# Delta rule: q and k of two head pairs projected channel-major together, their values token-major in 512 columns and convolved over tokens by shifted copies

## The chip, the cores and the metric

The kernel runs on one core of one Trainium2 chip. The time is the device time of one execution in microseconds (us), as the median of three runs. The engines are TensorE (PE in the profile, with PEld for its weight loads), VectorE (DVE), ScalarE (ACT), GpSimd (POOL) and SyncE (SP), which issues nearly all DMAs.

## The reference

One decoder layer on 256 tokens and 2048 channels, in float32. Two branches, a gated delta rule (GDN) and an mLSTM, are projected from the same `h`, gated, merged and projected out. What the change touches is the first part of the GDN branch:

```python
h = rms_norm(x, norm_pre_w) * (1 + scale) + shift
proj = h @ w_in                                   # (256, 2048) @ (2048, ...)
def causal_conv_silu(x, w):                       # 4 taps over tokens, per channel
    xp = jnp.pad(x, ((0, 0), (3, 0), (0, 0)))
    return silu(sum(xp[:, j:j + s] * w[j] for j in range(4)))
qkv = causal_conv_silu(gdn_qkv, gdn_conv_w)       # 8192 channels: q 16x128, k 16x128, v 32x128
q_a = l2_normalize(q) * 128 ** -0.5 ; k_a = l2_normalize(k)   # each shared by two value heads
g_log = -exp(A_log) * softplus(a + dt_bias) ; beta = sigmoid(b)
o_a = gated_delta_rule(q_a, k_a, v_a, g_log, beta)
o_a = rms_norm(o_a, gdn_norm_w) * silu(gdn_z)
```

## The kernel before

**Projections.** Every product in float32 is made of three float32r products: both operands are split into a high and a low part (`whi`, `wlo` of the weights, `h_hi`, `h_lo` of the tokens), and `mm3` issues high*high, high*low and low*high (L231). ACT casts the high part (L169), DVE subtracts for the low part (L170; in the start GpSimd does some). The weights stream through `Stream`: units of 1 MB (`raw`, 3 buffers, loaded by SP at L164), each split in two pieces of 1024 columns (`whi`, `wlo`, 4 buffers each). A piece is split up to four pieces ahead of its use on PE.

There are two forms. `add_proj_t` (PSUM tiles `pt`) gives channels on partitions: the weights are the stationary operand and the 256 tokens move, so a group of 512 columns of `w_in` takes 16 chunks x 4 x 3 = 192 matmuls of 128x256. `add_proj_n` (tiles `pn`) gives tokens on partitions: the tokens are stationary and 512 weight columns move, 16 x 2 x 3 = 96 matmuls of 128x512 for a group of the same size. Either group has four units, so eight pieces.

**The GDN stage** has 8 periods (`gdn_period`), each of two head pairs. A pair is one key head and two value heads, and its 512 columns (q, k, v, v) are one group of `w_in`. A period projects pair 0 with `add_proj_t`, the gates z of four heads with `add_proj_n`, and pair 1 with `add_proj_t`.

**Side work.** Everything else is written as Python generators in `side`; after each piece on PE `side.step()` lets every generator issue its next portion, so a `yield` is one piece. A budget (`side.debt`, `side.room`) spreads DVE work. Each engine works its own instructions in the order in which they were issued. The generators of a period:

- `gdn_stage1` per pair: `conv_silu` convolves the four channel blocks in place in `qs` (ACT scales the last tap at L650, DVE adds three shifted taps each at L656, ACT Silu at L659); q and k are split (`qh`, `ql`); the decay rows are loaded (`gb`, L674) and masked on GpSimd (`dd`, L681); PE makes the scores `psa` and `psb`, transposes q into `psb` (L715) and the two value heads into `psv` (L720) so that tokens come on partitions; DVE scales the scores into `au` (L748); ACT scales the values out of `psv` into `rr` (L761).
- `base_inverse` per period: the unit lower triangles are inverted in 32x32 blocks, by a chain of small DVE instructions (`tmp`, `xx`, L799 to L805) between DMA round trips through DRAM (`ud`, `ug`, `xd`, `xcmp`).
- `gdn_stage2` per period, about a period later: products with the inverse, the output, its norm and gate, the transposes back, and the store to `o_dr`.

Of the kernel before, what the change touches and what calls it, by code (L numbers as in the profile page):

```python
# [117 lines left out]
def hybrid_layer_kernel(  # L118
# [402 lines left out]
    def gates(ps):  # L521
# [53 lines left out]
        yield from wait(3)  # L575
# [34 lines left out]

    def add_proj_t(g, after, extra=None):

        st_ = {}
        for t in range(4):
# [9 lines left out]
            stream.add(w_in[g][:, t * 2048:(t + 1) * 2048], prep_w, use, after=  # L624
# [4 lines left out]
    def add_proj_n(g, after, extra=None):  # L629

        st_ = {}
        for t in range(4):
            def use(h, hi, lo, t=t):
                if t == 0 and h == 0:
                    st_["ps"] = [jtile(f"pn{i}") for i in range(2)]
                for kc in range(2):
                    k = t * 4 + h * 2 + kc
                    o = kc * 512
                    for b in range(2):
                        mm3(st_["ps"][b], h_hi[:, k, b * P:(b + 1) * P], h_lo[:, k, b * P:(b + 1) * P],  # L640
                            hi[:, o:o + 512], lo[:, o:o + 512], k == 0, k == KC - 1)
            stream.add(w_in[g][:, t * 2048:(t + 1) * 2048], prep_w, use, after=
                       (lambda: after(st_["ps"])) if t == 3 else None)
            if extra:
                extra()

    def conv_silu(ps, taps, dst, hi=None, late=0):
# [3 lines left out]
        yield from wait(1 + late)  # L651
# [8 lines left out]
        if hi is not None:  # L660
            A.copy(hi, dst[:, 0:2])
# [31 lines left out]
    def gdn_stage1(p, ps, res):  # L693

        z = p % 2
        qs = bp.tile([P, 4, S], F32, name="qs", tag="qs")
        qh = bp.tile([P, 2, S], F32R, name="qh", tag="qh", bufs=1)
        yield from conv_silu(ps, lambda n, j: late_c["gcv"][:, (p * 4 + n) * 4 + j:(p * 4 + n) * 4 + j + 1], qs, qh,
                             0 if z else 3)
        gb = decay_rows(2 * p)  # L700
        dd = decay_mask(gb)
        b12 = bp.tile([P, 2], F32, name="b12", tag="b12")
        G.tensor_tensor(b12, gb[:, :, P - 1], ngt[:, 0, 2 * p:2 * p + 2], op=ALU.add)
        side.debt += 0.7
        ql = bp.tile([P, 2, S], F32R, name="ql", tag="ql", bufs=1)
        V.tensor_tensor(ql, qs[:, 0:2], qh.bitcast(F32), op=ALU.subtract)
        yield from wait(2)
        yield from banks(3)
        res["t"] = side.t
        psa = gtile("psa", True)  # L710
        mm3(psa, qh[:, 1, 0:P], ql[:, 1, 0:P], qh, ql, True, True)
        psb = gtile("psb", True)
        mm3(psb[:, 0:256], qh[:, 1, P:S], ql[:, 1, P:S], qh[:, :, P:S], ql[:, :, P:S], True, True)
        for m in range(2):
            T.transpose(psb[:, 256 + m * P:256 + (m + 1) * P], qs[:, 0, m * P:(m + 1) * P], ident)  # L715
        psv = gtile("psv", True)
        side.debt -= 1.6
        for blk in range(2):
            for h in range(2):
                T.transpose(psv[:, (blk * 2 + h) * P:(blk * 2 + h + 1) * P],  # L720
                            qs[:, 2 + h, blk * P:(blk + 1) * P], ident)
# [6 lines left out]
        if z == 0:
            res["eq"] = bp.tile([P, 2, 2], F32, name="eq", tag="eq", bufs=3)
            res["rr"] = bp.tile([P, 2, 2, S], F32, name="rr", tag="rr")  # L730
        rk = bp.tile([P, 2], F32, name="rk", tag="rk")
        cj = bp.tile([P, 2, 2], F32, name="cj", tag="cj")
        res["au", z] = au = bp.tile([P, 2, 768], F32, name="au", tag="au", bufs=5)

        side.debt += 1.3
        for blk, ps_, n, c0 in ((0, psa, 256, 0), (1, psb, 128, 512)):
            V.scalar_tensor_tensor(au[:, 0, c0:c0 + P], ps_[:, n:n + P], 1.0, ident, op0=ALU.mult, op1=ALU.mult,
                                   accum_out=sse[:, 2 + blk:3 + blk])
        V.tensor_scalar(sse[:, 2:4], sse[:, 2:4], EPS, None, op0=ALU.add)
        V.reciprocal(rk, sse[:, 2:4])  # L740
        V.tensor_tensor(cj, tt[:, :, 32 + 2 * p:34 + 2 * p], rk.unsqueeze(2).broadcast_to([P, 2, 2]), op=ALU.mult)
        V.tensor_scalar(res["eq"][:, z], sse[:, 0:2], EPS, 128.0 * EPS, op0=ALU.add, op1=ALU.mult)

        for blk, ps_, n, c0 in ((0, psa, 256, 0), (1, psb, 128, 512)):
            yield
            side.debt += 1.45 if blk == 0 else 1.0
            for h in range(2):
                V.scalar_tensor_tensor(au[:, h, c0:c0 + 2 * n].rearrange("p (a b) -> p a b", a=2),  # L748
                                       ps_[:, 0:2 * n].rearrange("p (a b) -> p a b", a=2), cj[:, blk, h:h + 1],
                                       dd[:, h, c0 // 2:c0 // 2 + n].unsqueeze(1).broadcast_to([P, 2, n]),  # L750
                                       op0=ALU.mult, op1=ALU.mult)
            gfree(ps_)
            if blk == 0:
                sk = bp.tile([P, 2], F32, name="sk", tag="sk")
                pow_(sk, sse[:, 2:4], phalf[:, 0:2])
            else:
                scored[0] = p
        block_rows(res, z)
# [16 lines left out]
    def base_inverse(zg, res, zr):  # L775
# [48 lines left out]
        while zg < 7 and side.t < res["t"] + STAGE2_STEPS - 1:  # L824
# [142 lines left out]
    def period_tail(zg, ps, res, zr):  # L967
        yield from gdn_stage1(2 * zg + 1, ps, res)
        yield
        side.add(base_inverse(zg, res, zr), 2)  # L970

# [502 lines left out]
```

## Time and profile before

| what | value |
|---|---|
| median of three runs | 1596.39 us (1596.14 to 1596.67) |
| span of the profiled execution, first to last instruction | 1595.6 us |
| the profiled execution's own time beside its span | not given apart; the median lies 0.8 us above the span |
| PE / PEld / DVE / ACT / POOL busy | 99 / 87 / 72 / 59 / 15% |
| GDN stage | from 336.9 to 991.5 us, in steady state 81.62 us a period |
| memory traffic | 372.37 MB, mean 233 GB/s |

The durations of matmuls in the profile overlap, since matmuls are pipelined: a sum of them is more than the time that they take, and the distance from start to start tells their pace. A queue's letter q after an engine's name (SPq) marks DMAs issued by it.

### The profile page before, as it was taken

The numbers are of one execution on the slowest core, as the hardware profiler recorded it, in microseconds if no ns is written. First come the engines' busy times: TensorE is split into PE (matmuls) and PEld (weight loads), VectorE is DVE, ScalarE is ACT, GpSimd is POOL, SyncE is SP. The second block draws the span as 40 slices with busy tenths as digits, with TensorE's granted clock in tenths as the row PEclk, the third lists the DMA queues.
The fourth block names the chain that finished last, engine by engine and source line by source line (L and its number), as shares of the span: only waits on it lengthen the run. The fifth ranks groups of instructions, "written<-read, shape, count | busy, mean of one in ns | idle before, by whom it ended". The sixth has DMA issues, their size and how long they took to land.

```text
span 1595.6 us, 25488 instructions
## 1 busy us (share of the span) xinstructions
PE 1581.1 (99%) x9854; PEld 1388.9 (87%) x9854; DVE 1145.7 (72%) x1804; ACT 937.7 (59%) x1496; POOL 244.8 (15%) x204
## 2 busy tenths in 40 slices
PE   8999999999999999999999999999999999999998
PEld 5888888899999999999999999889988888888886
DVE  6786556765689788888878888775768766756654
ACT  7754446765666575757576766665566554444443
POOL 4787761000000010000000000000000000100100
PEclk9999999999999999999999999999999999999999
DMA  9998775965555546555646455546778878776573
GB/s 379 390 385 324 267 296 179 298 233 182 187 192 186 190 151 202 172 184 172 195 157 206 155 193 177 187 165 228 280 271 306 321 277 294 282 249 236 207 270 111
DMA packets 96067, 372.37 MB, mean 233 GB/s; under 512 B 26021, under 2 KB 45877, under 8 KB 58185
## 3 DMA queue, kind: packets, MB, share of 16 engines
q1 hardware_dynamic: 95848, 370.65, 65.7%
q8 instruction: 77, 1.26, 0.3%
q14 instruction: 44, 0.36, 0.1%
q0 software_dynamic: 96, 0.09, 0.0%
q10 hardware_dynamic: 2, 0.01, 0.0%
HBM read 354.40 MB, written 16.31 MB: 232 GB/s over the span
## 4 chain that ended last, share of the span: by engine, by line
PE 82%; issue 13%; ACT 1%; DMA 1%; POOL 1%; DVE 1%; SPq 0%; DVEq 0%; POOLq 0%; ACTq 0%
PE pn L231 37%; PE pt L231 28%; PE py L231 8%; POOL mg L1264 1%; PE psa L231 1%; PE mq L871 1%; PE mz L880 1%; ACT whi L169 0%; DVE wlo L170 0%; DMA gb<-rows 0%; PE csil L301 0%; PE po L921 0%; PE po L920 0%; PE pa L892 0%; PE pc L910 0%
## 5 line engine op out<-in xcount | busy, mean ns | idle before, releaser
L170 DVE TENSOR_TENSOR wlo<-raw,whi 128x1024 fp32r<-128x1024 f32 x453 | 555.9, 1235 | 266.5 <-ACT whi L169 265.2
L169 ACT CAST whi<-raw 128x1024 fp32r<-128x1024 f32 x516 | 532.2, 1046 | 308.5 <-PE pn L231 156.3
L231 PE MATMUL pt<-h_hi,whi 128*128 128x256 f32 x1280 | 367.8, 287 | 0.0
L231 PE MATMUL pt<-h_hi,wlo 128*128 128x256 f32 x1280 | 362.1, 283 | 0.0
L231 PE MATMUL pt<-h_lo,whi 128*128 128x256 f32 x1280 | 362.0, 283 | 0.0
L231 PE MATMUL pn<-whi,h_hi 128*128 128x512 f32 x896 | 353.0, 394 | 0.9 <-ACT part L474 0.6
L231 PE MATMUL pn<-wlo,h_hi 128*128 128x512 f32 x896 | 349.2, 390 | 0.9 <-POOL wlo L170 0.9
L231 PE MATMUL pn<-whi,h_lo 128*128 128x512 f32 x896 | 349.1, 390 | 0.0
L231 PEld LDWEIGHTS pt<-h_hi,whi 128*128 128x128 f32 x1280 | 245.3, 192 | 1.4
L231 PEld LDWEIGHTS pt<-h_lo,whi 128*128 128x128 f32 x1280 | 245.4, 192 | 0.3
L231 PEld LDWEIGHTS pt<-h_hi,wlo 128*128 128x128 f32 x1280 | 245.2, 192 | 0.0
L231 PEld LDWEIGHTS pn<-whi,h_hi 128*128 128x128 f32 x896 | 168.3, 188 | 36.4 <-ACT part L474 1.5
L231 PEld LDWEIGHTS pn<-wlo,h_hi 128*128 128x128 f32 x896 | 168.3, 188 | 35.8 <-POOL wlo L170 1.7
L231 PEld LDWEIGHTS pn<-whi,h_lo 128*128 128x128 f32 x896 | 168.2, 188 | 35.3 <-DVE h_lo L170 0.2
L170 POOL TENSOR_TENSOR wlo<-raw,whi 128x1024 fp32r<-128x1024 f32 (+1 forms) x63 | 145.7, 2319 | 50.5 <-ACT whi L169 50.4
L231 PE MATMUL py<-whi,yhi 128*128 128x512 f32 x384 | 150.6, 392 | 0.0
L231 PE MATMUL py<-whi,ylo 128*128 128x512 f32 x384 | 149.6, 390 | 0.0
L231 PE MATMUL py<-wlo,yhi 128*128 128x512 f32 x384 | 149.4, 389 | 0.0
L472 DVE TENSOR_TENSOR part<-pn,part 128x512 f32<-128x512 f32 x112 | 73.7, 685 | 45.5 <-PE pn L231 45.4
L169 ACT CAST yhi<-ya 128x512 fp32r<-128x512 f32 x48 | 29.9, 622 | 127.1 <-PE py L231 110.5
L656 DVE SCALAR_TENSOR_TENSOR qs<-pt,gcv,qs 128x255 f32<-128x255 f32 (+2 forms) x192 | 92.0, 479 | 4.6
L170 DVE TENSOR_TENSOR ylo<-ya,yhi 128x512 fp32r<-128x512 f32 x48 | 33.2, 691 | 74.2 <-ACT yhi L169 74.2
(267 smaller groups left out, 1807.0 us busy)
## 6 DMA issues: line engine op xcount, KB each, us to landing
raw<-in_dram SPq DMA_DIRECT2D x259, 1024.0 KB
ar<-in_dram SPq DMA_DIRECT2D x31, 1024.0 KB
raw<-in_dram SPq DMA_DIRECT2D x16, 512.0 KB
ya<-o_dr SPq DMA_DIRECT2D x32, 256.0 KB
gate_dr<-part SPq DMA_DIRECT2D x11, 512.0 KB
gb<-rows SPq DMA_DIRECT2D x20, 256.0 KB
raw<-in_dram SPq DMA_DIRECT2D x6, 768.0 KB
ug<-ud SPq DMA_DIRECT2D x32, 128.0 KB
```

What stands on the lines that cost most here:

```text
L169: A.copy(hi, src)
L170: (eng or V).tensor_tensor(lo, src, hi.bitcast(F32), op=ALU.subtract)
L231: T.matmul(ps, l, r, start=start and i == 0, stop=stop and i == 2, skip_group_check=True)
L472: V.tensor_tensor(part[g][:, b], ps[b], part[g][:, b], op=ALU.add)
L656: V.scalar_tensor_tensor(dst[:, n, sh:], src[:, 0:S - sh], taps(n, 3 - sh), dst[:, n, sh:], op0=ALU.mult, op1=ALU.add)
L871: T.matmul(psp[64:128, m * 64:(m + 1) * 64], um(m)[0:64, 64:128], y0[:, m], start=True, stop=True)
L880: T.matmul(psz[0:64, m * 64:(m + 1) * 64], p2[64:128, m], x0[64:128, m, 64:128], start=True, stop=True)
L1264: G.tensor_tensor(mcols(b, hf, cg), mcols(b, hf, cg), s_, op=ALU.add)
```

## The change

Lines of the kernel after are some higher than before (the split is at L173, `mm3` at L234, `load_w` at L165 and L167).

A period now projects q and k of both pairs in one `add_proj_t` group (512 channels: q0, k0, q1, k1), the four value heads of both pairs in one `add_proj_n` group (512 columns, tokens on partitions), and then z. The columns are taken by `columns` out of the two pairs' groups of `w_in`, so such a 1-MB unit is loaded by two DMAs of 512 KB with runs of 1 KB. `gdn_stage1` now serves both pairs, one after the other, and has no `psv`. The values get their own generator `gdn_values`: their convolution runs over partitions now, so the tokens are stored to DRAM (`vd`, with three rows of zeros ahead) and read back three times, shifted by one to three rows; the taps, which now vary along the free dimension, come from a transposed copy of the convolution weights in DRAM (`conv_dr`), broadcast to all partitions. GpSimd multiplies and adds two of the four taps, DVE the other two, and DVE adds the halves.

```diff
-    def conv_silu(ps, taps, dst, hi=None, late=0):
+    def conv_silu(ps, taps, dst):
...
+    def columns(g, t, half):
+        if isinstance(g, int):
+            return w_in[g][:, t * 2048:(t + 1) * 2048]
+        return tuple(w_in[i].rearrange("p (k c) -> p k c", c=512)[:, 4 * t:4 * t + 4, half * S:(half + 1) * S] for i in g)
...
+        for i, s_ in enumerate(src if isinstance(src, tuple) else (src,)):
+            if len(s_.shape) == 3:
+                SP.dma_start(raw.rearrange("p (k g c) -> p k g c", k=4, g=2)[:, :, i], s_)
...
     def gdn_period(zg):
         res = {}
-        add_proj_t(2 * zg, lambda ps: side.add(gdn_stage1(2 * zg, ps, res)))
+        pair = (2 * zg, 2 * zg + 1)
+        add_proj_t(pair, lambda ps: side.add(gdn_stage1(zg, ps, res, zrs[zg])))
+        add_proj_n(pair, lambda ps: side.add(gdn_values(zg, ps, res)))
         add_z(zg)
-        add_proj_t(2 * zg + 1, lambda ps: side.add(period_tail(zg, ps, res, zrs[zg])))
...
-        psv = gtile("psv", True)
-        side.debt -= 1.6
-        for blk in range(2):
-            for h in range(2):
-                T.transpose(psv[:, (blk * 2 + h) * P:(blk * 2 + h + 1) * P],
-                            qs[:, 2 + h, blk * P:(blk + 1) * P], ident)
...
-        for blk in range(2):
-            A.activation(res["rr"][:, blk, z], psv[:, blk * S:(blk + 1) * S], AF.Copy, scale=sk[:, blk:blk + 1])
-        gfree(psv)
+    def gdn_values(zg, ps, res):
+        rr = bp.tile([P, 2, 2, S], F32, name="rr", tag="rr")
+        v = [yp.tile([P, 2, S], F32, name="v", tag="ya", bufs=3) for z in range(2)]
+        for z in range(2):
+            for b in range(2):
+                A.copy(v[z][:, b], ps[b][:, z * S:(z + 1) * S])
+        yield
+        for z in range(2):
+            w = []
+            for i in range(2):
+                w.append(yp.tile([P, 2, S], F32, name="cw", tag="ylo", bufs=2))
+                SP.dma_start(w[i], conv_dr[2 * zg + z, 2 * i:2 * i + 2, 2:4].rearrange("t n c -> t (n c)")
+                             .unsqueeze(0).broadcast_to([P, 2, S]))
+            SP.dma_start(vd[z, 3:].rearrange("(b t) c -> t b c", b=2), v[z])
+            yield from wait(2)
+            vs = [v[z]]
+            for j in range(1, 4):
+                vs.append(yp.tile([P, 2, S], F32, name=f"v{j}", tag="ya" if j == 3 else "yhi", bufs=3 if j == 3 else 2))
+                SP.dma_start(vs[j], vd[z, 3 - j:3 - j + S].rearrange("(b t) c -> t b c", b=2))
+            yield from wait(2)
+            def tap(e, j):
+                e.tensor_tensor(vs[j], vs[j], w[(3 - j) // 2][:, (3 - j) % 2].unsqueeze(1).broadcast_to([P, 2, S]),
+                                op=ALU.mult)
+            tap(G, 3)
+            tap(G, 2)
+            G.tensor_tensor(vs[2], vs[2], vs[3], op=ALU.add)
+            side.debt += 1.4
+            tap(V, 0)
+            tap(V, 1)
+            yield
+            V.tensor_tensor(vs[0], vs[0], vs[1], op=ALU.add)
+            yield
+            V.tensor_tensor(vs[0], vs[0], vs[2], op=ALU.add)
+            yield
+            A.activation(rr[:, :, z], vs[0], AF.Silu)
+            while ("sk", z) not in res:
+                yield
+            yield
+            for b in range(2):
+                A.activation(rr[:, b, z], rr[:, b, z], AF.Copy, scale=res["sk", z][:, b:b + 1])
+        res["rr"] = rr
```

Once, in the start (`gates`), the convolution weights are regrouped by one DVE copy, transposed by two PE transposes, copied by ACT and stored, and the zero rows of `vd` are stored.

**PE, at the scores of one pair in a steady period.** Before (`psa`, `psb` scores, `psv` the transposed values, `pt` the running projection):

```order
L231 MATMUL psa_6000<-qh_5603 128x512
L231 MATMUL psa_6000<-ql_5899,qh_5603 128x512
L231 MATMUL psa_6000<-qh_5603,ql_5899 128x512
L231 MATMUL psb_6004<-qh_5603 128x256
L231 MATMUL psb_6004<-ql_5899,qh_5603 128x256
L231 MATMUL psb_6004<-qh_5603,ql_5899 128x256
L715 MATMUL psb_6004<-con_76,qs_5602 128x128 x2
L720 MATMUL psv_6010<-con_76,qs_5602 128x128 x4
L231 MATMUL pt0_5833<-h_hi_87,whi_5827 128x256
L231 MATMUL pt0_5833<-h_lo_88,whi_5827 128x256
```

After:

```order
L234 MATMUL psa_5820<-qh_5690 128x512
L234 MATMUL psa_5820<-ql_5732,qh_5690 128x512
L234 MATMUL psa_5820<-qh_5690,ql_5732 128x512
L234 MATMUL psb_5824<-qh_5690 128x256
L234 MATMUL psb_5824<-ql_5732,qh_5690 128x256
L234 MATMUL psb_5824<-qh_5690,ql_5732 128x256
L741 MATMUL psb_5824<-con_76,qs_5496 128x128 x2
L234 MATMUL pn0_5799<-whi_5699,h_hi_87 128x512
L234 MATMUL pn0_5799<-wlo_5700,h_hi_87 128x512
```

The four transposes of the values (L720) are gone, and the scores now stand inside a group of 512 columns.

**DVE, where the convolution of the values was and is.** Before, in pair 1's group (`qs` rows of L656 are three taps of one channel block; the same three follow for each of four blocks):

```order
L748 SCALAR_TENSOR_TENSOR au_5630<-psb_5581,cj_5629,dd_5496 128x256 x2
L170 TENSOR_TENSOR wlo_5682<-raw_5511,whi_5681 128x1024
L656 SCALAR_TENSOR_TENSOR qs_5602<-pt0_5264,gcv_1719,qs_5602 128x255
L656 SCALAR_TENSOR_TENSOR qs_5602<-pt0_5264,gcv_1719,qs_5602 128x254
L656 SCALAR_TENSOR_TENSOR qs_5602<-pt0_5264,gcv_1719,qs_5602 128x253
L170 TENSOR_TENSOR wlo_5703<-raw_5511,whi_5702 128x1024
L656 SCALAR_TENSOR_TENSOR qs_5602<-pt0_5264,gcv_1719,qs_5602 128x255
L656 SCALAR_TENSOR_TENSOR qs_5602<-pt0_5264,gcv_1719,qs_5602 128x254
```

After (`v`, `v1` the unshifted and the once shifted tokens, `cw` the taps, `v2` the sum that GpSimd made; `ql` and `so` belong to the scores and to stage 2):

```order
L173 TENSOR_TENSOR wlo_5004<-raw_4778,whi_5003 128x1024
L732 TENSOR_TENSOR ql_5038<-qs_4521,qh_4923 128x512
L806 TENSOR_TENSOR v_4829<-v_4829,cw_4881 128x512
L806 TENSOR_TENSOR v1_4951<-v1_4951,cw_4881 128x512
L173 TENSOR_TENSOR wlo_5052<-raw_4842,whi_5051 128x1024
L1002 SCALAR_TENSOR_TENSOR so_4987<-so_4987,eq_3177 128x8
L816 TENSOR_TENSOR v_4829<-v_4829,v1_4951 128x512
L173 TENSOR_TENSOR wlo_5071<-raw_4842,whi_5070 128x1024
L819 TENSOR_TENSOR v_4829<-v_4829,v2_4953 128x512
L173 TENSOR_TENSOR wlo_5111<-raw_4932,whi_5110 128x1024
```

Six channel-major tap instructions a pair give way to two products and two sums of 128x512 a pair, spread over three pieces; the first waits for `cw`, the second for a DMA out of `vd`, the fourth for GpSimd.

**SP, the same part of a period.** Before (`raw` weights, `gb` decay rows, `ud`, `ug` blocks of the inverse, `o_dr` the output):

```order
L674 DMA gb_6483<-rows_92 128x512
L164 DMA raw_6500<-in_8_dram 128x2048
L164 DMA raw_6601<-in_8_dram 128x2048
L164 DMA raw_6650<-in_8_dram 128x2048
L772 DMA ud_6159<-au_6619 32x4x32 x4
L164 DMA raw_6695<-in_8_dram 128x2048
L965 DMA o_dr_146<-oT_6719 128x2x256
L965 DMA o_dr_146<-oT_6722 128x2x256
L781 DMA ug_6748<-ud_6159 32x1x1024 x4
```

After (`cw`, `vd`, `v1` to `v3` as above):

```order
L165 DMA raw_5074<-in_8_dram 128x4x256 x2
L165 DMA raw_5143<-in_8_dram 128x4x256 x2
L795 DMA cw_5182<-conv_dr_94 128x2x256
L795 DMA cw_5184<-conv_dr_94 128x2x256
L797 DMA vd_95<-v_4830 128x2x256
L837 DMA ud_4997<-au_5131 32x4x32 x4
L165 DMA raw_5237<-in_8_dram 128x4x256 x2
L802 DMA v1_5264<-vd_95 128x2x256
L802 DMA v2_5266<-vd_95 128x2x256
L802 DMA v3_5268<-vd_95 128x2x256
```

Two tap loads, a store and three loads come into the queue for each pair, between weight loads, and each weight load of q, k and v is issued as two DMAs.

More of the change, by code (lines that the diff above doesn't have):

```diff
@@ L162, in load_w @@
         c = 0
-        for s_ in src if isinstance(src, tuple) else (src,):
+        for i, s_ in enumerate(src if isinstance(src, tuple) else (src,)):
+            if len(s_.shape) == 3:
+                SP.dma_start(raw.rearrange("p (k g c) -> p k g c", k=4, g=2)[:, :, i], s_)
+                continue
             SP.dma_start(raw[:, c:c + s_.shape[1]], s_)
@@ L574, in gates @@
         SP.dma_start(rows[32:40], mm_[64:72])
-        yield from wait(3)
+        for z in range(2):
+            SP.dma_start(vd[z, 0:3], zz[0:3])
+        yield from wait(1)
+        gct, gcp = t_("gct"), t_("gcp")
+        V.tensor_copy(gcp.rearrange("c (p t n) -> c p t n", n=4, t=4),
+                      late_c["gcv"].rearrange("c (p n t) -> c p t n", n=4, t=4))
+        tc_ = gtile("tc")
+        for b in range(2):
+            T.transpose(tc_[:, b * P:(b + 1) * P], gcp[:, b * P:(b + 1) * P], ident)
+        A.copy(gct, tc_[:, 0:S])
+        yield from wait(2)
+        for b in range(2):
+            SP.dma_start(conv_dr[8 * b:8 * b + 8].rearrange("p t n c -> (p t n) c"), gct[:, b * P:(b + 1) * P])
         tp = gtile("tp")
@@ L623, in use @@
                             h_hi[:, k], h_lo[:, k], k == 0 and n % 2 == 0, k == KC - 1 and n % 2 == 1)
-            stream.add(w_in[g][:, t * 2048:(t + 1) * 2048], prep_w, use, after=
+            stream.add(columns(g, t, 0), prep_w, use, after=
                        (lambda: after(st_["ps"])) if t == 3 else None)
@@ L641, in use @@
                             hi[:, o:o + 512], lo[:, o:o + 512], k == 0, k == KC - 1)
-            stream.add(w_in[g][:, t * 2048:(t + 1) * 2048], prep_w, use, after=
+            stream.add(columns(g, t, 1), prep_w, use, after=
                        (lambda: after(st_["ps"])) if t == 3 else None)
@@ L691, in decay_exp, with gdn_stage1 @@
             A.activation(dd[:, h, S:384], dd[:, h, S:384], AF.Exp, bias=b22[:, h:h + 1])
-    def gdn_stage1(p, ps, res):
-        z = p % 2
+    def gdn_stage1(zg, ps, res, zr):
         qs = bp.tile([P, 4, S], F32, name="qs", tag="qs")
+        yield from conv_silu(ps, lambda n, j: late_c["gcv"][:, (8 * zg + 4 * (n // 2) + n % 2) * 4 + j:
+                                                            (8 * zg + 4 * (n // 2) + n % 2) * 4 + j + 1], qs)
+        res["eq"] = bp.tile([P, 2, 2], F32, name="eq", tag="eq", bufs=3)
@@ L697, in gdn_stage1 @@
         qh = bp.tile([P, 2, S], F32R, name="qh", tag="qh", bufs=1)
[L698 to L715, printed above, removed]
@@ L727, in gdn_stage1 @@
-        yield
[L728 to L744, printed above, removed]
-            yield
[L746 to L757, printed above, removed]
@@ L823, in base_inverse @@
         yield
-        while zg < 7 and side.t < res["t"] + STAGE2_STEPS - 1:
+        while "rr" not in res or zg < 7 and side.t < res["t"] + STAGE2_STEPS - 1:
             yield
@@ L965, in gdn_stage2 @@
             SP.dma_start(o_dr[4 * zg + 2 * z:4 * zg + 2 * z + 2].rearrange("h d t -> d h t"), oT)
[L967 to L970, printed above, removed]
     zrs = [{} for _ in range(8)]
```

75 lines of the change are left out of this document (66 added, 9 removed).

## The prediction

> **What bounds the kernel now.** I began with the page: busy time, slices and the chain of work that ended last.
>
> ```profile
> span 1595.6 us, 25488 instructions
> PE 1581.1 (99%) x9854; PEld 1388.9 (87%) x9854; DVE 1145.7 (72%) x1804; ACT 937.7 (59%) x1496; POOL 244.8 (15%) x204
> ...
> PE   8999999999999999999999999999999999999998
> ...
> DVE  6786556765689788888878888775768766756654
> ...
> PEclk9999999999999999999999999999999999999999
> ...
> PE 82%; issue 13%; ACT 1%; DMA 1%; POOL 1%; DVE 1%; SPq 0%; DVEq 0%; POOLq 0%; ACTq 0%
> ```
>
> The reader is to see that PE is busy in every slice at full clock, and that the chain is PE's own work; DVE, at 80% in most slices of the GDN stage (the 12th to the 25th), comes next. So what PE is spared shows in the time, as long as DVE keeps ahead of it. Matmul durations overlap, so I took the pace from the timeline, at the first GDN group, where nothing is inserted: the first matmul of a channel-major group, of the token-major group behind it, and of the next group. The windows view between them shows no idle PE. Its last row here is a steady period.
>
> ```profile
> 336.90 0.28 PE L231 MATMUL pt<-h_hi,whi 128*128 128x256 f32 x1
> ...
> 359.94 0.40 PE L231 MATMUL pn<-whi,h_hi 128*128 128x512 f32 x1
> ...
> 381.73 0.28 PE L231 MATMUL pt<-h_hi,whi 128*128 128x256 f32 x1
> ...
> 336.90:359.94 23.04, 23.04 (x194) 23.03 (x192) 12.49 (x12) 10.19 (x12) 1.42 (x2) 1.00 0.66 234
> 359.94:381.73 21.79, 21.79 (x99) 18.02 (x98) 15.22 (x20) 9.90 (x13) 0.00 (x0) 1.00 0.52 183
> 746.66:828.28 81.62, 81.62 (x675) 76.65 (x674) 67.23 (x140) 53.16 (x98) 4.49 (x7) 1.00 0.55 179
> ```
>
> 192 matmuls of 256 columns took 23.04 us (120 ns each), 96 of 512 columns 21.79 us (227 ns each), for the same number of weights. In the first group the weight loads (PEld, third figure) fill the window, 23.03 us; in the second they leave 3.8 us free. In a steady period PE is busy for all of 81.62 us, DVE for 67.23, ACT for 53.16, POOL for 4.49.
>
> **The change, part by part.**
>
> *Projection form.* Each period swaps one channel-major group for a token-major one: 23.04 - 21.79 = 1.25 us, on PE, which is the bound; 8 periods give **10.0 us**. The Trainium skill (TensorE: Matmul & The Clock Gate, Back-to-back issue gap) gives an isolated gap of N/2.4 + 2.5 ns, so 109 ns and 216 ns here; an estimate by that page makes the swap worth 0.25 us, 2.0 us in all, but the rows above have 120 and 227 ns.
>
> *Transposes of the values.* They go, four a pair.
>
> ```profile
> 701.63 0.39 PE L715 MATMUL psb<-con,qs 128*128 128x128 f32 x2
> 701.85 0.60 PE L720 MATMUL psv<-con,qs 128*128 128x128 f32 x4
> 702.21 0.36 PE L231 MATMUL pt<-h_hi,whi 128*128 128x256 f32 x1
> ```
>
> From their start to the next matmul are 0.36 us; by the two transposes ahead (0.22 us) four are 0.44. Between these ends, which differ by the last one's overlap, I take 0.40; 16 pairs give **6.4 us** (5.8 to 7.0). Against it stand two transposes in the start, by the same rows 0.2 us, once; they follow a DVE copy of the same step without a yield, which may hold PE for up to the copy's length. I add nothing for that.
>
> *DVE and ACT work.* These rows price it (the 691-ns row has both inputs in SBUF, as the new products have).
>
> ```profile
> L656 DVE SCALAR_TENSOR_TENSOR qs<-pt,gcv,qs 128x255 f32<-128x255 f32 (+2 forms) x192 | 92.0, 479 | 4.6
> L170 DVE TENSOR_TENSOR ylo<-ya,yhi 128x512 fp32r<-128x512 f32 x48 | 33.2, 691 | 74.2 <-ACT yhi L169 74.2
> L650 ACT ACTIVATE qs<-pt,gcv 128x256 f32<-128x256 f32 x64 | 25.1, 485 | 3.7 <-PE pt L231 3.7
> L659 ACT ACTIVATE qs<-qs 128x1024 f32<-128x1024 f32 x16 | 17.0, 1060 | 16.7 <-DVE qs L656 16.5
> L979 ACT ACTIVATE sz<-pn 128x512 f32<-128x512 f32 x16 | 8.8, 595 | 1.1 <-PE pn L231 1.0
> L1041 ACT COPY hn<-pnum 128x256 f32<-128x256 f32 x16 | 5.8, 364 | 0.0
> ```
>
> DVE a period: 12 taps go (12 x 0.479 = 5.7 us), 8 products and sums come (8 x 0.691 = 5.5): 0.2 us less. ACT: 4 scalings and one Silu go (1.9 + 1.06), 4 copies of `v` and 2 Silus of 512 come (1.5 + 1.2), so 0.3 us less; the scaling into `rr` stays. Both lie beside PE: 0 us.
>
> *GpSimd beside DVE.* Six instructions of 128x512 a period come onto a nearly idle engine. The trace has GpSimd products of that size beside DVE splits in the merge:
>
> ```profile
> 1369.67 7.54 POOL L1264 TENSOR_TENSOR mg<-mg,gs 128x512 f32<-128x512 f32 x4 [120.89 <-DMA ya<-o_dr]
> ...
> 1369.96 2.07 DVE L170 TENSOR_TENSOR wlo<-raw,whi 128x1024 fp32r<-128x1024 f32 x1
> ...
> 1373.76 4.54 DVE L170 TENSOR_TENSOR wlo<-raw,whi 128x1024 fp32r<-128x1024 f32 x2
> ...
> 730.79 1.22 DVE L170 TENSOR_TENSOR wlo<-raw,whi 128x1024 fp32r<-128x1024 f32 x1
> ...
> 733.53 0.28 PE L231 MATMUL pt<-h_hi,whi 128*128 128x256 f32 x1
> ```
>
> Three splits beside four products took 2.07 + 4.54 = 6.61 us instead of 3 x 1.22 = 3.66: 2.95 us lost, 0.74 a GpSimd instruction. Six a period would cost DVE 4.4 us (bounds: 0 if they fall beside work out of PSUM, 11.3 if DVE stood still for all of 6 x 7.54/4). DVE then has 67.2 - 0.2 + 4.4 = 71.4 us of work in a period of about 79.6; with the upper end 78.3, still below. So 0 us on average. The Trainium skill (SBUF — State Buffer, Who interferes with whom) says that a DVE instruction with two SBUF inputs and a GpSimd instruction that reads SBUF exclude each other; the splits above agree in direction. An estimate from the upper end, 11.3 us, is what full exclusion would be, and that too leaves PE the bound of the period; what it can do at one place is the first rival.
>
> The place to watch is the last two rows: the split that PE needed at 733.53 ended at 732.01, a lead of 1.5 us, behind the inverse (L799 to L805) and the tap instructions of pair 1. After, the inverse stands beside the taps of the next q and k, and the scores of both pairs stand elsewhere, so its stretch is not heavier; the value products come ahead of it, among pieces with little else, where a lost microsecond can be made up. I leave the lead at 1.5 us or better.
>
> *New waits.* DVE and GpSimd now wait for a trip through DRAM: store `vd`, then three loads. Nearest rows: decay rows behind weights, and the inverse's trip.
>
> ```profile
> 693.93 0.38 SPq L674 DMA_DIRECT2D gb<-rows  x1
> ...
> 700.13 0.99 POOL L681 TENSOR_SCALAR_AFFINE_SELECT dd<-gb 128x256 f32<-128x256 f32 x2 [27.96 <-DMA gb<-rows]
> ...
> SPq L812 <- DMA xd<-xx: 17.8, 8, 4.9
> ```
>
> A load of 256 KB behind weights took 6.2 us from issue to use; the inverse's store was waited for 2.2 us on average, 4.9 at most. Two steps of 3.3 us (79.6/24 pieces) lie between store and loads, two more to the first product: 13.2 us. Needed are four copies of `v` (1.5), a store and loads (2.2 to 6.2 each) and three issues (3 x 0.38): 7.0 to 15.0 us. So DVE waits at most 1.8 us at L806. Behind it on DVE stands the next split, for which PE waits; its lead covers that, and pair 1's store needs no copies. Behind GpSimd's products stand the norm's power `so` and the next masks, used a step or more later. Price 0; both ends go into the range.
>
> *DMA.* A period gets 12 DMAs of 256 KB and 8 more issues for the same weights: 3.1 MB on 81.62 x 179 = 14.6 MB, so 223 GB/s. SP issues 20 more at 0.38 us, 7.6 us, beside waits. Runs of 1 KB are read by the late projections now, and there PE does not idle:
>
> ```profile
> 1230.00:1498.00 268.00, 267.89 (x1192) 220.27 (x1191) 175.34 (x184) 132.37 (x177) 9.38 (x5) 1.00 0.76 274
> ```
>
> DMA engines were busy 76% at 274 GB/s and PE 267.89 of 268.00 us. Hidden: weights are asked for two units ahead.
>
> **Sum.** -10.0 - 6.4 + 0.2 = -16.2 us. The span of the profiled execution becomes 1579.4; the median lies 0.8 us above that span, so **1580.2 us**. If only the price ends of the transposes vary, 1579.6 to 1580.8; another 2 us each way for stalls that go (a few tenths a period) or come at the group borders: 1578 to 1583.
>
> **Rivals.**
> 1. *GpSimd delays DVE where its lead is thin.* If half of the 4.4 us fall into the inverse's stretch, the lead of 1.5 us is overdrawn by 0.7, and PE idles 8 x 0.7 = 5.6 us: 1585.8. With all of it, 8 x 2.9 = 23 us: no faster. For it: the splits of 2.07 us. Against it: the products are issued ahead of the inverse. This is also how full exclusion would act.
> 2. *Slower: the trip through DRAM comes late and DVE stands.* Place: L806 of each pair. With a wait of 3.0 us where the lead is 1.5, PE loses 1.5 for each of 16 pairs, 24 us: 1604. It turns from faster to slower at a wait of 1.5 + 16.2/16 = 2.5 us a pair. For it: 15.0 us needed at worst against 13.2. Against it: the lead is thin only behind the inverse.
> 3. *Width buys nothing: the change doesn't do what it says.* If 512 columns among inserted work took as long as two times 256, 240 ns, the first term would be 0 and the time 1590.2. Against it: both paces stand in the rows, and z has the wide form in every period. By the gap of the Trainium skill (TensorE: Matmul & The Clock Gate) 2.0 us of that term would be left, 1588.2.
>
> **How the numbers follow.** Forecast 0.74, rival 1 0.13 (a third of it no faster), rival 2 0.08, rival 3 0.02, something faster than 1578 0.03. I call 0.2% (3.2 us) what a measurement can tell from no change. Faster: 0.74 + 0.08 + 0.02 + 0.03 = 0.87; the rest of rivals 1 and 2 gives same 0.05 and slower 0.08. The range reaches from 1575 (2 us more stalls gone, transposes at the upper end) to 1590 (rival 1 with 10 us).
>
> **What would show it.** Right: 2304 `pt` and 3456 `pn` projection matmuls at 120 and 227 ns, a steady period of 79.6 us with PE busy all of it, no `psv`, DVE near 71 us a period, GpSimd products of 1.3 to 2.3 us. Wrong: PE idle before a weight load with the split as releaser; DVE waiting at the first value product for `vd` over 2 us; splits over 2 us inside the inverse.

## The result and the profile after

The change made the kernel slower: 1666.21 us median of 4 runs (1664.93 to 1668.28) against 1596.53 for the kernel before (1596.14 to 1596.97, 4 runs), a ratio of 1.0433 with a 95% interval of 1.0419 to 1.0448. That is 69.7 us more than before and 86.0 more than forecast. The profiled execution took 1666.84 us. Its page, in the parts shown of before (busy time, slices of PE and of the granted clock, the chain by engine):

```profile
span 1665.0 us, 24146 instructions
...
PE 1593.6 (96%) x9024; PEld 1360.4 (82%) x9024; DVE 1177.5 (71%) x1773; ACT 915.2 (55%) x1489; POOL 337.9 (20%) x252
...
PE   8999999899998998998989899999999999999998
...
PEclk9999999999999999999999999999999999999999
...
PE 54%; issue 14%; DVE 10%; DMA 10%; ACT 4%; POOL 3%; SPq 3%; DVEq 0%; POOLq 0%; ACTq 0%
```

PE falls below 9 in the 8th slice (the start) and in the 13th, 16th, 19th, 21st and 23rd (the GDN stage), and the chain, which was 82% PE, now runs through DVE, DMA, ACT, POOL and SP for 30% of the span. The windows view, for the first channel-major group and for a steady period:

```profile
344.15:367.19 23.04, 23.04 (x194) 23.03 (x193) 12.49 (x12) 10.19 (x12) 1.42 (x2) 1.00 0.71 235
751.50:844.60 93.10, 83.95 (x570) 73.95 (x569) 70.70 (x134) 50.84 (x98) 17.80 (x15) 0.95 0.62 191
```

Where nothing is inserted, the pace is that of before (23.04 us). A steady period takes 93.10 us instead of 81.62, PE is idle for 9.15 of them, and the granted clock of the stretch is 0.95 on the mean (the slices above, 42 us each, don't show it; the last section has one place). DMA engines are busy 62% at 191 GB/s: not full. The view of waits has what is new:

```profile
POOL v L806 <- DMA v<-vd: 169.4, 14, 17.9
DVE v L806 <- DMA v<-vd: 81.0, 15, 9.2
ACT rr L821 <- DVE v L819: 67.2, 13, 7.3
PEld pt L234 <- DVE wlo L173: 33.1, 11, 6.4
SPq L877 <- DMA xd<-xx: 45.3, 8, 6.9
```

DVE stands at L806, the value products, for the shifted copies (81.0 us in 15 waits, the longest 9.2), ACT then for DVE's sums, and PE before a weight load for the split (L173): two of the signs that the prediction named as "wrong". SP stands 45.3 us for the inverse's `xd`, where it was 17.8; 34.9 of that stay when the trip is left out (below), so most of the rise comes with the regrouping and costs little by itself. One place where DVE stands at L806, from the timelines of SP, of DVE and of PE, in that order (start, duration, instruction; in brackets the idle time ahead and what ended it):

```profile
828.41 0.93 SPq L165 DMA_DIRECT2D raw<-in_dram  x2
...
830.45 0.47 SPq L797 DMA_DIRECT2D vd<-v  x1
...
831.47 0.53 SPq L873 DMA_DIRECT2D xd<-xx  x1
838.93 2.75 SPq L877 DMA_DIRECT2D xcmp<-xd  x4
...
842.76 1.53 SPq L802 DMA_DIRECT2D v<-vd  x3
...
839.30 0.68 DVE L806 TENSOR_TENSOR v<-v,cw 128x512 f32<-128x512 f32 x1
848.55 0.69 DVE L806 TENSOR_TENSOR v<-v,cw 128x512 f32<-128x512 f32 x1 [8.57 <-DMA v<-vd]
849.16 1.22 DVE L173 TENSOR_TENSOR wlo<-raw,whi 128x1024 fp32r<-128x1024 f32 x1
...
850.44 0.58 PE L234 MATMUL pt<-h_hi,wlo 128*128 128x256 f32 x1 [5.45 <-DVE wlo L173]
```

ACT's copies of `v` had ended at 822.16; SP came to the store only at 830.45, since it stood until 828.41 at a weight load whose buffer was still in use. Then it stood at L877 until `xd` had landed, and issued the three loads at 842.76, 12.3 us after the store. DVE had been at the second product since 839.98, 9.5 us after the store, and got on at 848.55. The split behind it came late, and PE idled 5.45 us.

### The profile page after: what moved, and what is told of

The parts are those of the page before. It is cut to its first block, busy times and chain, and to the rows that moved or that the text cites. A ratio compares the mean times of both kernels' runs of the same rounds, so it can differ in the third digit from the quotient of the medians.

```text
span 1665.0 us, 24146 instructions
## 1 busy us (share of the span) xinstructions
PE 1593.6 (96%) x9024; PEld 1360.4 (82%) x9024; DVE 1177.5 (71%) x1773; ACT 915.2 (55%) x1489; POOL 337.9 (20%) x252
## 3 DMA queue, kind: packets, MB, share of 16 engines
q1 hardware_dynamic: 180628, 395.96, 69.2%
## 4 chain that ended last, share of the span: by engine, by line
PE 54%; issue 14%; DVE 10%; DMA 10%; ACT 4%; POOL 3%; SPq 3%; DVEq 0%; POOLq 0%; ACTq 0%
PE pn L234 33%; PE py L234 8%; PE pt L234 8%; DMA v<-vd 4%; DVE wlo L173 4%; DMA vd<-v 2%; ACT whi L172 2%; POOL v L806 1%; DMA xd<-xx 1%; DVE on L1016 1%; DMA raw<-in_dram 1%; DVE tmp L864 1%; DMA ud<-au 1%; DVE qs L679 1%; DVE xx L868 1%
## 5 line engine op out<-in xcount | busy, mean ns | idle before, releaser
L173 DVE TENSOR_TENSOR wlo<-raw,whi 128x1024 fp32r<-128x1024 f32 x453 | 567.7, 1262 | 191.5 <-ACT whi L172 190.3
L234 PE MATMUL pn<-whi,h_hi 128*128 128x512 f32 x1152 | 463.2, 402 | 1.2 <-ACT part L479 0.6
L234 PE MATMUL pn<-wlo,h_hi 128*128 128x512 f32 x1152 | 453.8, 394 | 3.1 <-DVE wlo L173 1.8
L234 PE MATMUL pn<-whi,h_lo 128*128 128x512 f32 x1152 | 453.5, 394 | 0.0
L234 PEld LDWEIGHTS pn<-wlo,h_hi 128*128 128x128 f32 x1152 | 219.3, 190 | 49.0 <-DVE wlo L173 3.5
L234 PEld LDWEIGHTS pn<-whi,h_hi 128*128 128x128 f32 x1152 | 219.1, 190 | 47.4 <-ACT part L479 1.5
L234 PEld LDWEIGHTS pn<-whi,h_lo 128*128 128x128 f32 x1152 | 218.8, 190 | 47.4
L234 PE MATMUL pt<-h_hi,wlo 128*128 128x256 f32 x768 | 223.1, 291 | 30.8 <-DVE wlo L173 30.8
L234 PE MATMUL pt<-h_hi,whi 128*128 128x256 f32 x768 | 223.9, 291 | 0.0
L234 PE MATMUL pt<-h_lo,whi 128*128 128x256 f32 x768 | 221.6, 289 | 0.0
L234 PEld LDWEIGHTS pt<-h_hi,wlo 128*128 128x128 f32 x768 | 152.0, 198 | 33.1 <-DVE wlo L173 33.1
L173 POOL TENSOR_TENSOR wlo<-raw,whi 128x1024 fp32r<-128x1024 f32 (+1 forms) x63 | 145.6, 2319 | 51.1 <-ACT whi L172 51.0
L234 PEld LDWEIGHTS pt<-h_hi,whi 128*128 128x128 f32 x768 | 151.9, 198 | 0.8
L234 PEld LDWEIGHTS pt<-h_lo,whi 128*128 128x128 f32 x768 | 151.9, 198 | 0.5
L234 PE MATMUL py<-whi,yhi 128*128 128x512 f32 x384 | 150.6, 392 | 0.0
L234 PE MATMUL py<-whi,ylo 128*128 128x512 f32 x384 | 149.5, 389 | 0.0
L234 PE MATMUL py<-wlo,yhi 128*128 128x512 f32 x384 | 149.5, 389 | 0.0
L806 POOL TENSOR_TENSOR v<-v,cw 128x512 f32<-128x512 f32 x32 | 51.0, 1612 | 197.2 <-DMA v<-vd 169.4
```

Of the source, the lines that this page charges most:

```text
L173: (eng or V).tensor_tensor(lo, src, hi.bitcast(F32), op=ALU.subtract)
L234: T.matmul(ps, l, r, start=start and i == 0, stop=stop and i == 2, skip_group_check=True)
L806: e.tensor_tensor(vs[j], vs[j], w[(3 - j) // 2][:, (3 - j) % 2].unsqueeze(1).broadcast_to([P, 2, S]), op=ALU.mult)
```

## Experiments

All start from the kernel after the change unless an edit says otherwise; all were timed beside the kernel before, which stood at 1596.5 to 1596.8 us each time.

### The regrouping alone, and the first theories

**Without the trip** (`e1_no_trip`).

```
-   (loads of cw, store vd, loads v<-vd, four products, three sums)
+   vs = [v[z]]; yield from wait(7)
```

> Leaves out the value convolution: no shifted copies through DRAM, no taps, no loads of the weights of the taps; the values go from their copy to the Silu, after as many steps. The regrouping of the projections and their split loads in 1-KB runs stay. Theory (the copies come late, DVE stands at the second product of L806 and the splits behind it stand too): 1580 to 1588 us, no PE gaps over 2 us at the pt groups, only the 4.4 us at the transposes in the start stay. Rival 'weights': the split loads in 1-KB runs come late themselves; then 1640 us or more, and ACT waits for raw as long as after the change (30 us). Rival 'GpSimd': its products hold DVE off; it would give 1580 to 1588 as well, since they go too.

1589.09 us, ratio 0.9951 (0.9936 to 0.9966). A steady period, from the first matmul of one channel-major group to that of the next, has PE busy without a pause:

```profile
719.66:799.48 79.82, 79.82 (x570) 70.71 (x569) 62.06 (x126) 50.69 (x99) 7.65 (x9) 1.00 0.60 184
```

79.82 us against the forecast 79.6 and 81.62 before. So the regrouping does what the prediction's sum says, and the split weight loads don't stop it; the loss belongs to the trip. PE has 570 matmuls in this period and 570 in the steady period after the change: those take 83.95 us of PE there and 79.82 here. So of the 13.3 us between 93.10 and 79.82, 9.15 are idle PE and 4.1 are the same matmuls at a slower pace. The stop of PE in the start stayed (4.2 us in the list, 4.4 in my expectations).

**Contiguous weights** (`e2_contig`), **more steps** (`e3_late`), **early stores** (`e4_store_early`).

```
e2: -  w_in[i]...[:, 4t:4t+4, half*S:(half+1)*S] for i in g     +  w_in[g[half]][:, t*2048:(t+1)*2048]
e3: -  yield from wait(2)   (loads to products)                 +  yield from wait(5 - z)
e4: -  SP.dma_start(vd[z, 3:], v[z])                            +  A.dma_start(...), behind ACT's copies of v
```

> The weights of two pairs are laid out so that q and k of both and the values of both are each one 1-MB load in 8-KB runs; all else as after the change. Theory 'late copies': 1648 to 1665 us, since the order of SP's queue and the trip stay; at most the loads of the copies land 1 to 2 us sooner. Rival 'weights': 1580 to 1600 us. Rival 'GpSimd': 1660 to 1667 us.

> Between the loads of the copies and the first product stand 5 steps for a first pair and 4 for a second one, where there were 2; nothing else. Theory 'late copies': DVE comes to the products 16.6 us (6.7 + 3 steps of 3.3) and 13.3 us after the store, where the copies were there after 17 to 18.6 us and 12.8 to 13.5 us; about 1.5 us of wait stay in 8 pairs, inside DVE's lead: 1584 to 1605 us. Rival 'weights': 1655 to 1670 us. Rival 'GpSimd': 1655 to 1670 us.

> The stores of both pairs' values are issued by ACT behind its copies, 8 us (first pairs) and 40 us (second pairs) before SP came to them; the loads stay on SP where they were. Theory 'late copies', by its two halves: in the second pairs the loads find the store landed, go out about 6 us sooner and DVE's wait there (about 6 us) all but goes; in the first pairs of the later periods the loads still stand behind SP's wait for xd (L877) and come 12 us after the weights of the taps, so that wait stays: 1610 to 1640 us. If the two transfers themselves were the cost and not SP's order, the first pairs would gain too: 1585 to 1600 us. Rival 'GpSimd' or 'weights': 1660 to 1670 us.

1657.24 us (ratio 1.0386, 1.0369 to 1.0404), 1634.51 (1.0232, 1.0216 to 1.0247) and 1658.50 (1.0387, 1.0371 to 1.0402). Contiguous loads are worth 9 us: the rival "weights" falls. Early stores alone bring 8, not the 26 and more that I expected: the loads stayed at their place in SP's order, and in the second pairs they came just as DVE came. With more steps no wait of DVE for copies is left in its list, and yet 1634 is 30 to 50 us above what I expected. Something else stands in its place, from the waits of `e3_late`:

```profile
DVE nsu L853 <- DMA ug<-ud: 29.6, 5, 6.8
DVE nsu L853 <- DMA v<-vd: 10.8, 2, 7.2
```

`nsu` is the first work of the inverse, and `ug` the blocks that it reads, which make a trip through DRAM of their own. `nsu` doesn't read the copies; `ug` and the copies use the same few semaphore numbers (last section), so the second row may be waits for `ug` too. My theory of one cause fell there.

### What the transfers cost where nobody reads them

**DVE's taps out** (`e8_no_dve_taps`), **all taps out** (`e10_traffic_only`), **GpSimd's work alone** (`e12_gpsimd_only`).

```
e8:  -  tap(V, 0); tap(V, 1); V adds          (G's two products and sum stay)
e10: -  all products and sums                 (stores, loads, cw stay)
e12: -  stores, loads, cw, DVE's taps         +  G: two products and a sum on v[z] itself
```

> Stores, loads, tap weights and GpSimd's products and addition stay as after the change; DVE's two products and two additions of a pair are left out, so DVE and ACT wait for no copy. Theory 'late copies': the time of the kernel without the trip, 1587 to 1596 us. Rival 'collateral' (more transfers make other transfers late): 1605 to 1630 us. Rival 'GpSimd' (its products beside DVE hold DVE off): 1605 to 1665 us, with DVE's splits longer than 1.23 us on the mean.

> Stores, loads and tap weights stay as after the change, and all products and additions of the taps are left out, on GpSimd and DVE. Of the 40 us by which the kernel with GpSimd's taps alone (1629) stands above the one without the trip (1589), theory 'other transfers come late' leaves nearly all: 1618 to 1630 us; theory 'GpSimd holds DVE off' nearly nothing: 1589 to 1600 us; both: between.

> No trip and no tap weights; GpSimd does two products and an addition of the same size for each pair on values that lie on the chip, at about the same steps; DVE's taps are left out. Theory 'GpSimd holds DVE off': 1605 to 1629 us; theory 'other transfers come late': 1588 to 1594 us.

1629.14 us (ratio 1.0199, 1.0182 to 1.0216), 1627.26 (1.0191, 1.0171 to 1.0211), 1593.76 (0.9982, 0.9972 to 0.9991). Against 1589.09 without the trip: transfers alone cost 38.2 us, GpSimd's work alone 4.7, both 40.1; all three times lie in the ranges of the theory that other transfers come late. How transfers that no engine waits for can stop PE is read from the timelines. First SP without the trip, then SP with the transfers alone, then DVE, ACT and PE of the latter:

```profile
728.88 2.52 SPq L810 DMA_DIRECT2D ud<-au  x4
...
733.55 3.24 SPq L819 DMA_DIRECT2D ug<-ud  x4
```

```profile
755.54 1.27 SPq L797 DMA_DIRECT2D vd<-v  x1
756.91 2.01 SPq L822 DMA_DIRECT2D ud<-au  x4
760.36 1.03 SPq L165 DMA_DIRECT2D raw<-in_dram  x2
...
763.00 2.50 SPq L802 DMA_DIRECT2D v<-vd  x3
765.54 2.62 SPq L831 DMA_DIRECT2D ug<-ud  x4
...
776.86 0.14 DVE L838 TENSOR_SCALAR nsu<-ug 128x15 f32<-128x15 f32 x1 [8.01 <-issue]
...
779.64 1.04 ACT L172 CAST whi<-raw 128x1024 fp32r<-128x1024 f32 x1 [5.03 <-DVE tmp L849]
780.71 0.58 ACT L931 COPY x<-mz 64x512 f32<-64x512 f32 x1
...
781.34 1.16 PE L942 MATMUL pa<-rr,x 128*128 128x128 f32 x8 [1.81 <-ACT x L931]
```

From the store of the blocks to their load SP took 4.7 us without the trip and 8.6 with it (over the eight periods 2.9 to 4.7 and 6.9 to 9.9): the copies' loads stand between. DVE, in order, stood 8.0 us at `nsu` (the profile puts the end of this one wait down to `issue`, and names `ug` in the other seven); ACT's cast waited for DVE, the copy `x` stood behind the cast, and PE waited for `x`. Such waits for `ug` add up in the lists (kernel before, without the trip, transfers alone):

```profile
DVE nsu L788 <- DMA ug<-ud: 2.2, 2, 1.2
```

```profile
DVE nsu L826 <- DMA ug<-ud: 9.8, 6, 2.6
```

```profile
DVE nsu L838 <- DMA ug<-ud: 60.3, 7, 10.1
```

**Another queue** (`e13_pool_traffic`), **another place in the queue** (`e14_order_traffic`), both on the transfers alone.

```
e13: -  SP.dma_start(cw / vd / v)       +  G.dma_start(...)
e14: +  yield from wait(2 * z)          (second pair's block behind ug's load)
```

> The kernel with the transfers alone (1627 us: stores, loads and tap weights, no products), with these transfers issued by GpSimd, on a queue of their own, instead of SP. Theory 'SP's queue' (the other round trips and the weights stand behind them in SP's order): 1589 to 1600 us, and DVE's wait for the blocks of the inverse (60 us) goes. Theory 'the traffic itself' (3 MB more a period in 1-KB runs make every transfer slower): 1615 to 1630 us.

> The kernel with the transfers alone, with those of each second pair 2 steps later, so that on SP they stand behind the load of the inverse's blocks (ug) instead of ahead of it (6 issues and two landings); the bytes are the same. Theory 'ug comes late': DVE's 60 us of wait at nsu fall below 25 us and the time to 1595 to 1612 us. Theory 'the traffic itself', and theory 'the weights come late': 1618 to 1630 us.

1591.55 us (ratio 0.9971, 0.9959 to 0.9982) and 1611.91 (1.0093, 1.0078 to 1.0108). The same bytes on GpSimd's queue cost 2.5 us, so it isn't the traffic but SP's queue. DVE's wait for `ug` did not go, though I had expected that; it fell from 60.3 to 29.8 us. Moving the second pairs' transfers behind `ug` gave 15.4 of the 35.7 us; the time forecast for that theory, 1612 at most, was just met, the wait (44.1 us where I had said below 25) was not. What makes up the other 20 us was not taken apart. The weights are a candidate: ACT waits 78.6 us for `raw` there and 79.5 before the transfers were moved, but 19.3 on the other queue and 12.5 without the trip. SP's list shows a second way of standing in the queue beside order: its weight loads wait for landings of copies, which they don't use (`L165 <- v<-vd`, 18.1 us in 31 waits with the transfers alone, 10.0 in 19 in `e14_order_traffic`, none on GpSimd's queue). No run separates the two.

**The move off SP's queue, with everything computed** (`e19_pool_only`): the edit of `e13_pool_traffic`, with all products.

> As after the change, with all products, and only the queue changed: the stores, loads and tap weights of the trip are issued by GpSimd. If the two costs add (the transfers in SP's queue 36 us, DVE's stand for the copies 37 us), 1625 to 1637 us, with DVE still standing 4 to 6 us a pair, since loads and products are 2 steps apart and a store and a load take 11 to 13 us one after the other. If SP's queue was also what made the copies late, 1595 to 1612 us.

1629.24 us, ratio 1.0205 (1.0188 to 1.0222): 37.0 less than the changed kernel, the time forecast for costs that add. The waits are not as forecast:

```profile
DVE v L806 <- DMA v<-vd: 34.6, 6, 6.1
```

DVE stands for copies in six of the second pairs only, and no longer in the first pairs: its stand fell from 81.0 to 34.6 us with the queue alone. So SP's queue was also what made the first pairs' copies late, and the two costs are not separate stands. The other 40 us against the kernel without the trip were not taken apart; PE's longest wait there is 13.4 us in all for ACT's `p` in the block solve.

### Other queues, places and engines

**ACT's queue** (`e5_act_queue`), **the same with 4 steps** (`e6_act_late`), **the same with contiguous weights and a yield in the start** (`e7_all`).

```
e5: -  SP.dma_start(vd / v)      +  A.dma_start(...)
e6: e5, and wait(2) -> wait(4) between loads and products
e7: e6, e2's layout, and in the start:  V.tensor_copy(gcp, ...);  +  yield;  T.transpose(...)
```

> Stores and loads of the copies are issued by ACT, on a queue with nothing else in it, at the same steps; SP's queue keeps the rest. Theory 'late copies by SP's queue': SP's order holds nothing up (12 us before the loads of first pairs) and the loads don't stand behind 1-MB weights in one queue (6 to 7 us from issue to landing): DVE, which comes about 6.5 us after the store, waits 0 to 2 us; 1592 to 1615 us. Rival 'the transfers themselves are slow, whatever the queue': 1640 to 1660 us. Rival 'ACT stands for the store's landing before it issues the loads': ACT's whi come late instead, PE gaps at whi, 1620 to 1650 us.

> As the kernel with ACT's queue, and 4 steps instead of 2 between loads and products. Theory 'late copies': no wait of DVE for copies left; forecast for the regrouping 1589 (the kernel without the trip) plus DVE's and GpSimd's taps and ACT's issues, that is 1588 to 1600 us. Rival 'collateral' (the extra small transfers make other transfers late, such as the blocks of the inverse, for which DVE stood 7 us when only the steps were added): 1610 to 1635 us.

> As the last one, with the weights of two pairs contiguous (1 MB in 8-KB runs) and one step between DVE's copy of the tap weights in the start and their transposes. Theory: the 4.4 us of the start go, and what the split loads cost (9 us after the change): 1578 to 1590 us. Rival 'collateral': 1600 to 1625 us.

1636.85 us (ratio 1.0242, 1.0221 to 1.0263), 1628.03 (1.0199, 1.0184 to 1.0215), 1619.90 (1.0143, 1.0126 to 1.0160): each in the range of a rival. The rival's mechanism is not shown for the first: PE waits only 2.3 us for `whi` there, and 13.2 for `ql`. ACT's queue doesn't free SP's: in the waits of `e7_all`, SP's issue of `ug` stands for landings of ACT's copies, which it doesn't use:

```profile
SPq L847 <- DMA v<-vd: 20.2, 11, 5.9
```

The yield cut PE's stop in the start from 4.2 to 1.5 us.

**All taps on DVE**, from the changed kernel (`e9_dve_taps`) and from the last one (`e11_all_dve`).

```
-  tap(G, 3); tap(G, 2); G add
+  tap(V, 2); tap(V, 3); V add
```

> GpSimd does none of the taps: DVE does its two products and the addition as well (3 x 0.68 us more for a pair, 4.1 us a period), in the same steps; all else as after the change. Theory 'GpSimd holds DVE off' (after the change DVE's operations beside GpSimd's lasted 39 us longer in all than elsewhere, before it 6 us): that goes, and DVE's own 33 us more fall where it stands for the copies anyway or not: 1640 to 1660 us. Theory 'late copies' and 'other transfers come late' alone: 1664 to 1685 us.

> The kernel with everything (ACT's queue, 4 steps, contiguous weights, a step in the start; 1620 us), with all taps on DVE. Theory 'GpSimd holds DVE off': DVE loses the 43 us that its operations there last longer beside GpSimd and gains 33 us of products, and its tight place ahead of psa (PE stands 2.5 to 2.7 us a period for ql) goes: 1595 to 1608 us. Otherwise, 1620 to 1635 us.

1647.47 us (ratio 1.0314, 1.0297 to 1.0330), 18.7 less than after the change and in the range of the theory; and 1633.35 (1.0224, 1.0209 to 1.0239), 13.5 more than `e7_all` and outside it. The sign depends on the kernel, so neither engine is the better one everywhere.

**Reordered** (`e15_reorder`): stores by ACT, a first pair's loads on SP ahead of `xd`, a second pair's behind `ug`, with the weights and the yield of `e7_all`.

> All values and taps computed. Stores by ACT behind its copies; loads and tap weights (one transfer of 512 KB instead of two) of a first pair go out on SP ahead of the inverse's xd, 5 steps ahead of the products; those of a second pair behind ug, 4 steps ahead; contiguous weights; one step in the start; one step more between the last addition and the Silu. Theory 'round trips in SP's order': no wait of DVE for copies, DVE's wait for ug under 15 us, 1583 to 1600 us. Theory 'the traffic itself': 1610 to 1625 us.

1618.11 us, ratio 1.0131 (1.0116 to 1.0146): above what I expected, and in the range given to the traffic itself, which had cost 2.5 us on GpSimd's queue. DVE waits under 1 us for copies in its list, and 9.7 us for `ug`; but PE waits for `ql`, 12.3 us in 5 periods. The timelines of POOL and DVE at that place, and behind them the same three operations of DVE without the trip:

```profile
724.58 1.39 POOL L806 TENSOR_TENSOR v<-v,cw 128x512 f32<-128x512 f32 x1
725.93 1.31 POOL L806 TENSOR_TENSOR vx<-vx,cw 128x512 f32<-128x512 f32 x1
727.32 1.61 POOL L810 TENSOR_TENSOR vx<-vx,v 128x512 f32<-128x512 f32 x1
...
723.67 2.45 DVE L1017 SCALAR_TENSOR_TENSOR on<-on,so,sz 128x128 f32<-128x128 f32 x4
726.04 1.75 DVE L733 TENSOR_TENSOR ql<-qs,qh 128x512 fp32r<-128x512 f32 x1
727.71 2.31 DVE L173 TENSOR_TENSOR wlo<-raw,whi 128x1024 fp32r<-128x1024 f32 x1
```

```profile
792.55 1.43 DVE L989 SCALAR_TENSOR_TENSOR on<-on,so,sz 128x128 f32<-128x128 f32 x4
793.90 0.68 DVE L732 TENSOR_TENSOR ql<-qs,qh 128x512 fp32r<-128x512 f32 x1
794.51 1.21 DVE L173 TENSOR_TENSOR wlo<-raw,whi 128x1024 fp32r<-128x1024 f32 x1
```

Beside GpSimd's three, DVE's take 2.45, 1.75 and 2.31 us instead of 1.43, 0.68 and 1.21: 3.2 us, in a stretch where DVE has no idle time. With the 12.3 us for `ql` some 17 of the 29.0 us above the kernel without the trip are not accounted for by these waits.

**That place relieved, and the transfers on GpSimd's queue**: all taps on DVE (`e17_pool_dve`), or only the first pair's (`e18_pool_mixed`).

> All values and taps computed. The order of the reordered kernel (1618 us), with loads and tap weights issued by GpSimd on its own queue (stores by ACT) and all taps on DVE. Theory 'SP's queue' and 'GpSimd holds DVE off at ql' together: no PE wait for ql (2.5 to 2.7 us a period there), ug as early as without the trip; 1584 to 1600 us. Rival 'DVE has no room for 9.5 us of taps a period': DVE's inverse ends late, PE waits for splits or mp; 1610 to 1635 us.

> As that, with GpSimd's two products and addition kept for the second pair of a period, and the first pair all on DVE, so that GpSimd's three operations no longer run beside the gating and ql. Theory: as above, 1584 to 1600 us; against the kernel with all on DVE, less by up to 5 us if the inverse beside the second pair is short of DVE, more by up to 5 us if GpSimd holds DVE off there. Rival 'the first pair's GpSimd work was not the cause of PE's wait for ql': PE still waits 2.5 us a period, 1605 to 1620 us.

1623.24 us (ratio 1.0173, 1.0150 to 1.0197) and 1597.27 (1.0002, 0.9993 to 1.0011). With all taps on DVE the inverse ends late, and PE waits for what follows it (`ycmp`, 15.1 us in 4 waits): the rival. The mixed kernel computes everything in the time of before, in the forecast range; PE's waits for `ql` fall to 2.0 us in all. It is 26.0 us below all taps on DVE, where I had expected 5 at most. It differs from the reordered kernel in the queue and in the first pair's engine, so the 20.8 us between them are not split. Its windows, for the third period and a steady one:

```profile
477.15:565.04 87.89, 82.57 (x561) 71.81 (x560) 73.48 (x139) 48.46 (x96) 17.34 (x19) 0.96 0.59 200
726.60:807.79 81.19, 80.40 (x569) 70.55 (x568) 70.26 (x138) 50.83 (x99) 17.23 (x20) 1.00 0.67 218
```

The steady period is a little shorter than before (81.62) and 1.4 us longer than without the trip. The third period loses 6.7 us more: in the first two PE has no block solve yet and runs through each in 69.2 us, and DVE, with the taps, needs 67.6 us for the first inverse (431.92 to the store of its result at 499.47), where a later one takes 46.7. That is read from its trace, not tested. No version that computes everything is faster than the kernel before.

## Why the prediction was wrong

- *Projection form and transposes, -16.4 us*: right but for 2 us. Without the trip a steady period is 81.62 - 79.82 = 1.80 us shorter, 14.4 us in 8 periods. The paces of 120 and 227 ns are those of the first groups after.
- *Start, +0.2 us*: mis-sized. PE stood 4.2 us for DVE's copy; I had named that copy and added nothing for it. A yield left 1.5. The first GDN group begins at 344.15 us instead of 336.90, and at 342.67 without the trip: 5.8 us late. So the kernel without the trip shows 7.4 us (1589.09 against 1596.53) of its 14.4.
- *New waits, 0 us*: **this step failed.** I wrote that the trip needs 7.0 to 15.0 us, that four steps give 13.2, and that DVE waits at most 1.8. The duration was about right in the second pairs, where DVE had its first shifted copy 11.4 to 13.5 us after the store, and too short in the later first pairs, with 16.9 to 18.6. The time on the other side was wrong. A step is an order, not a time: in the first pairs SP came to the store 4 to 10 us after the values were ready, and DVE, which runs ahead of PE by its splits, came to its products 6 to 13 us behind the store. And SP's queue was taken as free: in the first pairs the loads stood behind `xd`'s landing. DVE waited 81.0 us in 15 waits at L806, up to 9.2 at once, and its taps and its stand for the copies cost 37.1 us (1666.21 against 1629.14). That an idle PE is also slower afterwards (4.1 of the 13.3 us a period) was in no term.
- *The same step, what else is in the queue*: not asked at all. The transfers made the inverse's own trip late on the same queue; with the weights that came late this was 38.2 us, and 2.5 on another queue.
- *DMA, hidden*: right as far as it went. 191 GB/s, 62% busy; the bytes cost 2.5 us on GpSimd's queue. But I priced SP's 20 more issues as time beside waits, and what they cost was their place in the queue.
- *GpSimd beside DVE, 0 us*: mis-sized, and not the main cause. Alone 4.7 us, though in the changed kernel all taps on DVE are 18.7 us faster, so that GpSimd's part in it is not settled. At the tight place three GpSimd instructions cost DVE 3.2 us, 1.06 each, where I had taken 0.74. DVE's work in a steady period, 71.4 us by the sum, came out at 70.70. I had placed the value products away from thin stretches; in the reordered kernel they lay on one. The Trainium skill (SBUF — State Buffer, Who interferes with whom) says that a DVE instruction with two SBUF inputs and a GpSimd instruction that reads SBUF exclude each other; the traces agree in direction, 3.2 us lost to 4.3 of GpSimd's.
- *Rival 2* named the place, the mechanism and the sign, at 0.08 and with 24 us instead of 77 (1666.21 against 1589.09). Its "for", 15.0 us needed at worst, left out the queue's order, and its "against" looked for the thin lead only behind the inverse.

## What to carry to other kernels

A trip through DRAM is priced by what stands in its queue, both ways: list what the issuing engine waits for ahead of the trip's store and loads, and which other round trips now stand behind them. Steps of a hand-written order are no time: take from the trace when the in-order engine that consumes reaches the place, not when PE does. And to learn what a transfer costs, run it with nobody reading it, once in its queue and once in another.

## What the runs showed of the hardware

I had not expected transfers on ACT's queue to hold up SP. In the trace of `e7_all` the transfers of SP and ACT set the same eight semaphore numbers in turn, and an issue can wait for the number that it will set itself, so that SP's issue of `ug` waited 20.2 us in all for landings of copies issued by ACT. GpSimd's transfers set eight other numbers, and with the same transfers issued by GpSimd no wait of SP for `v<-vd` is listed. The numbering is this program's.

And an idle of PE cost more than its length. After the idle of 5.45 us shown above, 18 matmuls of 256 columns went at 0.21 us apart (850.82, 851.03, 851.24) instead of 0.12, from 850.44 to 854.40, and the granted clock of just that stretch was 0.50:

```profile
850.44:854.40 3.96, 3.96 (x18) 3.96 (x19) 3.96 (x4) 0.85 (x2) 3.64 (x3) 0.50 0.52 172
```

At 0.12 us they would take 2.2 us. Over the whole span the mean granted clock is 0.980 after the change, 0.999 before and 0.998 without the trip.
